# Fused high-weight matmul with a folded result, and every third low weight part on GpSimd

## The chip, the cores and the metric

The kernel runs on one core of a Trainium2 chip. The metric is the device time of one execution in microseconds (us); the time before is 1485.79 us, the median of three runs (1485.37 to 1486.06). Differences under 0.2% of it, 3 us, can hardly be told from no change.

Five engines work side by side, each through its own queue in order: TensorE (PE; its weight loads are listed as PEld), VectorE (DVE), ScalarE (ACT), GpSimd (POOL) and SyncE (SP), which here issues the DMAs. On-chip memory is SBUF, and PSUM for the results of matmuls; GpSimd works on SBUF alone in this kernel.

## The reference

Three transformer blocks on one sequence of 256 tokens with 1024 channels, all in float32: two layers of a first kind, one of a second. Cut to what matters:

```python
def first_block(x, ...):                      # two layers
    for l in range(2):
        h = rms_norm(x, norm1_g[l])
        (cq, ckv, kpe, gq, gk, gv, glr, gr, su, gates) = split_in(h @ w_in[l])     # 5808 columns
        o_a = mla_mixer(cq, ckv, kpe, ...)    # latent attention, 8 heads
        o_b = gla_mixer(gq, gk, gv, glr, gr, ...)   # gated linear attention
        o_c = s5_mixer(su, ...)               # state space scan, gelu, sigmoid-gated by y @ w_glu
        g = sigmoid(gates + gate_b[l]).reshape(B, L, 3, D)
        merged = g0 * (o_a @ w_br_mla) + g1 * (o_b @ w_br_gla) + g2 * (o_c @ w_br_s5)
        x = x + merged @ w_out[l]
        x = x + square(relu(rms_norm(x, norm2_g[l]) @ w_ff1[l])) @ w_ff2[l]        # 4096 hidden
def second_block(x, ...):                     # one layer
    q, k, v, glu_in, z_ga, z_gc = split(rms_norm(x, g_pre) @ w_in)
    y_attn = dilated_attention_mixer(q, k, v, rel_bias, w_attn_out)   # 3 groups of 8 heads
    y_conv = conformer_conv_mixer(glu_in, ...)   # glu, depthwise conv of width 31, norm, silu, w_conv_out
    x = x + rms_norm((sigmoid(z_ga) * y_attn + sigmoid(z_gc) * y_conv) @ w_mix_out)
    gate, up = split(rms_norm(x, g_pre_ffn) @ w_ffn_in)               # 2 x 2816
    x = x + rms_norm((silu(gate) * up) @ w_ffn_out)
```

## The kernel before

Every weight is read once, as a stream of 424 *units*. A unit is a tile `raw` of up to 128x1024 float32 (512 KB). To keep float32 accuracy, each unit is split into two parts of the type fp32r: ScalarE copies `raw` to the high part `wH` (`split`, L160), and VectorE subtracts to get the low part `wL = raw - wH` (L161). Activations are split in the same way (`hH` and `hL`, `fH` and `fL`, ...). A product of the two is three matmuls that add up in PSUM: high by high, high weight by low activation, low weight by high activation.

There are two kinds of product. In `mm_f` (L166) the weights are stationary, 128x128 at a time, and 256 tokens stream past: L169 (`hH` past `wH`), L170 (`hL` past `wH`), L171 (`hH` past `wL`). Output channels lie on partitions. A unit of `f_unit` has 8 such triples for 128 output channels: 24 matmuls of 256 columns into the first half of a PSUM tile `mm`. In `mm_t` (L173) the activations are stationary and 512 weight columns stream past (L175 to L177): the second matrices of the feed-forward parts (`ff2`, `ffo`), `w_out` and others, 12 matmuls of 512 columns to a unit.

The result of an `f_unit` is taken out of PSUM by its `evac`: mostly one ScalarE instruction that also does what comes next, as `Tanh` with a bias for the gates (`gate_evac`, L1038), `Relu` in the feed-forward part (`ff1`, L1190), `Tanh` or a bias for the two halves of the gated linear unit (`glu_gate` L1448, `glu_a` L1442). There are two `mm` tiles, taken in turn.

`fetch_` (L1773) issues a unit's DMA and its split; it runs three units ahead of the unit that is computed (`AHEAD`). The tile pools set what waits for what: three `raw` tiles, four `wH` and four `wL`, each taken in turn, so the DMA of unit i + 3 waits until the split of unit i has read `raw`, and the split of unit i + 4 until TensorE is done with unit i:

```python
    wraw = pool("wraw", 3)
    whl = pool("whl", 4)
    k.ps_mm = pool("ps_mm", 2, space=PS)
```

Twenty units have a factor per partition (`plan.scales`) and are split in two halves of 512 columns (L163, L164). The order of the units and of the side work beside them (the scan `s`, the attentions, the convolution `c`, the norms) stands in the tables `SCHED` and `SCHED2`. The convolution (`conv_gen`, L1250) is 31 taps over 256 tokens for eight channel tiles, on VectorE (`cv`, L1285 and L1278; ScalarE makes some products, `cvt`). GpSimd computes the powers -1/2 of the norms (`rsq`, L184) on at most 4 columns, and clears some tiles.

Of the kernel before, what the change touches and what calls it, by code (L numbers as in the profile page):

```python
# [150 lines left out]
def make(k, tc, ins, out, dbg=None):  # L151
    """Fills k with the helpers; returns the plan."""
# [132 lines left out]
def norm_full(k, t, rsn, ss, gb, dst):  # L285
    """rsn[:, t] = rsqrt(mean(x^2) + eps); the normed x into dst, transposed; gb holds g in every row."""
# [8 lines left out]

def row_tile(k, i, name):
# [5 lines left out]
def post_residual(k, t, accs, gb, eps=EPS * D):  # L302
    """x[:, t] += accs rsqrt(sum(accs^2) + eps) gb; gb holds sqrt(D) g."""
# [134 lines left out]
def s5_powers(k, st, name, nk, x, xs, ct, op):  # L438
    """[128, 8, nk, 16]: x times powers of lambda, for the four pairs of a channel tile, re and im."""
# [1502 lines left out]
```

## Time and profile before

| | |
|---|---|
| median of three runs | 1485.79 us |
| the profiled execution, span | 1482.4 us |
| PE busy | 1440.2 us (97%) |
| DVE busy | 1019.1 us (69%) |
| ACT busy | 840.1 us (57%) |
| POOL busy | 48.6 us (3%) |
| DMA | 243.13 MB, mean 164 GB/s |

The profile is of one execution; its own time is given as its span from the first to the last instruction, 1482.4 us, and the runs' median lies 3.4 us above that. In the rows below an instruction has the line of `kernel.py`, the engine, the tile that it writes and those that it reads, and its shape. Matmuls overlap in their records (one of 256 columns is shown as 0.28 us long, and the next one starts 0.12 us later), so a matmul's cost in a row of them is read from start to start. The same holds for VectorE, in a smaller measure.

### The profile page before, as it was taken

How to read it: one execution, taken by the hardware profiler on the slowest of the kernel's cores; microseconds unless marked ns; L12 is line 12 of the kernel's file. 1: busy time of each engine (PE TensorE's matmuls, PEld its weight loads, DVE VectorE, ACT ScalarE, POOL GpSimd, SP SyncE). 2: the span in 40 equal slices, each digit the busy share in tenths (PEclk: the TensorE clock that was granted, in tenths of full speed). 3: DMA queues.
4: the chain of work that ended last, by engine and by line, in shares of the span. 5: the costliest groups of instructions: out<-in, count | busy, mean ns of one | idle time of the engine just before them, and what ended most of it. 6: DMA issues, size and time to landing. Idle time of an engine off the chain costs nothing.

```text
span 1482.4 us, 26521 instructions
## 1 busy us (share of the span) xinstructions
PE 1440.2 (97%) x10580; PEld 1299.2 (88%) x10580; DVE 1019.1 (69%) x1876; ACT 840.1 (57%) x1469; POOL 48.6 (3%) x51
## 2 busy tenths in 40 slices
PE   8999999989999999989999999999999999899998
PEld 6979899778889899788988999989888989799997
DVE  7976777687455668566566555579988856765555
ACT  6855567465744556355546444465576574644443
POOL 1000100000000000012000000000000000000000
PEclk9999999999999999999999999999999999999999
DMA  6622344555455653235446555575544545355553
GB/s 223 207 86 97 108 162 152 163 171 183 160 165 186 209 165 94 81 130 171 155 164 218 189 185 186 188 234 178 179 146 121 167 143 206 126 195 185 185 185 114
DMA packets 71060, 243.13 MB, mean 164 GB/s; under 512 B 7864, under 2 KB 11656, under 8 KB 70936
## 3 DMA queue, kind: packets, MB, share of 16 engines
q1 hardware_dynamic: 70936, 241.43, 49.9%
q8 instruction: 83, 1.36, 0.4%
q14 instruction: 41, 0.34, 0.1%
HBM read 237.17 MB, written 4.23 MB: 163 GB/s over the span
## 4 chain that ended last, share of the span: by engine, by line
PE 72%; DVE 9%; ACT 3%; issue 2%; POOL 2%; DMA 1%; POOLq 0%; DVEq 0%; ACTq 0%; SPq 0%
PE mm L169 13%; PE mm L170 13%; PE mm L171 13%; PE acc L175 7%; PE acc L176 7%; PE acc L177 7%; DVE wL L161 3%; POOL rsq L184 2%; ACT wH L160 2%; DVE cv L1285 1%; PE acc L1409 1%; DMA raw<-in_wst_dram 1%; PE tr L1404 1%; PE acc L1382 1%; PE acc L548 1%
## 5 line engine op out<-in xcount | busy, mean ns | idle before, releaser
L161 DVE TENSOR_TENSOR wL<-raw,wH 128x1024 fp32r<-128x1024 f32 (+1 forms) x410 | 495.9, 1211 | 253.7 <-ACT wH L160 250.7
L160 ACT ACTIVATE wH<-raw 128x1024 fp32r<-128x1024 f32 (+1 forms) x410 | 429.2, 1047 | 379.7 <-PE mm L170 199.1
L169 PE MATMUL mm<-hH,wH 128*128 128x256 f32 x1920 | 553.5, 289 | 7.0 <-ACT gt L1038 3.5
L170 PE MATMUL mm<-hL,wH 128*128 128x256 f32 x1920 | 548.5, 286 | 3.2 <-DVE hL L164 3.2
L171 PE MATMUL mm<-hH,wL 128*128 128x256 f32 x1920 | 547.9, 286 | 0.0
L169 PEld LDWEIGHTS mm<-hH,wH 128*128 128x128 f32 x1920 | 368.5, 192 | 21.0 <-ACT hH L163 5.3
L170 PEld LDWEIGHTS mm<-hL,wH 128*128 128x128 f32 x1920 | 368.9, 192 | 8.8 <-DVE hL L164 4.4
L171 PEld LDWEIGHTS mm<-hH,wL 128*128 128x128 f32 x1920 | 368.9, 192 | 2.4 <-issue 1.9
L175 PE MATMUL acc<-wH,fH 128*128 128x512 f32 x344 | 135.3, 393 | 0.0
L176 PE MATMUL acc<-wL,fH 128*128 128x512 f32 x344 | 134.9, 392 | 0.0
L177 PE MATMUL acc<-wH,fL 128*128 128x512 f32 x344 | 134.1, 390 | 0.0
L1285 DVE SCALAR_TENSOR_TENSOR cv<-u,ppt,cv 128x256 f32<-128x256 f32 x184 | 78.6, 478 | 0.4
L177 PEld LDWEIGHTS acc<-wH,fL 128*128 128x128 f32 x344 | 64.6, 188 | 14.1
L175 PEld LDWEIGHTS acc<-wH,fH 128*128 128x128 f32 x344 | 64.9, 189 | 11.2
L176 PEld LDWEIGHTS acc<-wL,fH 128*128 128x128 f32 x344 | 64.9, 189 | 10.3
L160 ACT ACTIVATE fH<-ffr 128x256 fp32r<-128x256 f32 x64 | 26.6, 416 | 67.6 <-DVE ffr L1191 67.5
L161 DVE TENSOR_TENSOR fL<-ffr,fH 128x256 fp32r<-128x256 f32 x64 | 27.1, 424 | 23.2 <-ACT fH L160 23.2
L175 PE MATMUL acc<-wH,mH 128*128 128x512 f32 x96 | 37.9, 395 | 0.3 <-ACT mH L163 0.3
L176 PE MATMUL acc<-wL,mH 128*128 128x512 f32 x96 | 37.8, 394 | 0.0
L177 PE MATMUL acc<-wH,mL 128*128 128x512 f32 x96 | 37.2, 395 | 0.0
L184 POOL TENSOR_TENSOR rsq<-nm,mhalf 128x1 f32<-128x1 f32 x12 | 7.6, 635 | 841.5 <-DVE nm L223 841.5
L164 DVE SCALAR_TENSOR_TENSOR wL<-raw,ppt,wH 128x512 fp32r<-128x512 f32 x40 | 28.4, 747 | 9.1 <-ACT wH L163 9.1
(433 smaller groups left out, 2155.4 us busy)
## 6 DMA issues: line engine op xcount, KB each, us to landing
raw<-in_wst_dram SPq DMA_DIRECT2D x420, 512.0 KB, 3.4
xd<-x SPq DMA_DIRECT2D x6, 512.0 KB, 2.9
x<-xd SPq DMA_DIRECT2D x6, 512.0 KB, 4.3
bias<-bdram SPq DMA_DIRECT2D x8, 384.0 KB, 4.9
gnorm<-in_rows_dram SPq DMA_DIRECT2D x3, 512.0 KB, 5.1
raw<-in_wst_dram SPq DMA_DIRECT2D x4, 384.0 KB, 4.1
x<-in_x_dram SPq DMA_DIRECT2D x4, 256.0 KB, 3.3
x<-in_x_dram SPq DMA_DIRECT2D x2, 512.0 KB, 5.1
```

Source lines behind the costliest of these rows:

```text
L160: nc.scalar.activation(H, src, AF.Copy)
L161: nc.vector.tensor_sub(L, src, H)
L164: nc.vector.scalar_tensor_tensor(L, src, scale, H.bitcast(F32), op0=OP.mult, op1=OP.subtract)
L169: nc.tensor.matmul(ps, H[:, w], aH[:, i, :], start=(i == 0), stop=False)
L170: nc.tensor.matmul(ps, H[:, w], aL[:, i, :], start=False, stop=False)
L171: nc.tensor.matmul(ps, L[:, w], aH[:, i, :], start=False, stop=(i == nk - 1))
L175: nc.tensor.matmul(ps, aH[:, ki, tt], H[:, cols], start=start, stop=False)
L176: nc.tensor.matmul(ps, aH[:, ki, tt], L[:, cols], start=False, stop=False)
L177: nc.tensor.matmul(ps, aL[:, ki, tt], H[:, cols], start=False, stop=stop)
L184: nc.gpsimd.tensor_tensor(o, m, k.mhalf[:, 0:1].to_broadcast([P, n]), op=OP.pow)
L548: nc.tensor.matmul(ps[:, (4 * c + q) * 64:(4 * c + q + 1) * 64], E[:, c, :], us[:, q, :], start=True, stop=True)
L1285: nc.vector.scalar_tensor_tensor(st.cv[:, ct], u(ct, i), w(ct, i), st.cv[:, ct], op0=OP.mult, op1=OP.add)
```

## The change

`mm_p` takes the place of `mm_f` in all `f_unit`s, in the small unit `kg`, in the convolution's output and in the gate of the scan branch. The high and the low part of an activation now lie side by side in one tile (`h[:, i]` is 2 x 256 columns), and one matmul of 512 columns streams both past the high weights, into the two halves of the PSUM tile. The low weights add to the first half. `fold` then adds the halves: ScalarE copies the second half to SBUF (with the bias, where there is one), VectorE adds the first. What was one instruction on ScalarE with a function is now `fold` and the function after it. Scales of 1/8 are moved to where they cost nothing.

Of the weight units, every third one (number i with i mod 3 = 1) that has no factors gets its low part from GpSimd instead of VectorE. `SCHED`, `SCHED2`, the pools and the order of the weights stay. `mm_f` stays for the three branch matrices and the attention's output, `mm_t` as it was.

```diff
+    def mm_p(ps, H, L, a, nk, off=0, m=P):
+        for i in range(nk):
+            w = slice((off + i) * m, (off + i + 1) * m)
+            ai = a(i)
+            nc.tensor.matmul(ps, H[:, w], ai.rearrange("p b n -> p (b n)"), start=(i == 0), stop=False)
+            nc.tensor.matmul(ps[:, :S], L[:, w], ai[:, 0], start=False, stop=(i == nk - 1))
+
+    def fold(out, ps, bias=None, view=lambda a: a):
+        if bias is None:
+            nc.scalar.activation(out, view(ps[:, S:]), AF.Copy)
+        else:
+            nc.scalar.activation(out, view(ps[:, S:]), AF.Identity, bias=bias)
+        nc.vector.tensor_add(out, view(ps[:, :S]), out)
...
 def new_h(k):
-    hH = k.act.tile([P, 8, S], F32R, tag="hH", name="hH")
-    hL = k.act.tile([P, 8, S], F32R, tag="hL", name="hL")
-    return hH, hL
+    return k.act.tile([P, 8, 2, S], F32R, tag="h", name="h")
...
 def f_unit(k, plan, st, blocks, evac, nk=8):
     def run(H, L):
         ps = k.mm_tile()
-        k.mm_f(ps[:, :S], H, L, st.hH, st.hL, nk)
+        k.mm_p(ps, H, L, lambda i: st.h[:, i], nk)
...
-            nc.scalar.activation(st.gt[b, n // 2][:, n % 2], ps[:, :S], AF.Tanh, scale=0.5,
-                                 bias=k.pp("gateb", l)[:, i:i + 1])
+            g = st.gt[b, n // 2][:, n % 2]
+            k.fold(g, ps)
+            nc.scalar.activation(g, g, AF.Tanh, scale=0.5, bias=k.pp("gateb", l)[:, i:i + 1])
...
     def ff1(n):
         def evac(ps):
             r = k.t1("ffr")
-            nc.scalar.activation(r, ps[:, :S], AF.Relu)
-            nc.vector.tensor_mul(r, r, r)
+            k.fold(r, ps)
+            nc.vector.scalar_tensor_tensor(r, r, 0.0, r, op0=OP.max, op1=OP.mult)
...
+LOW_POOL = 3
...
+        elif i % LOW_POOL == 1:
+            nc.scalar.activation(H[:, :n], raw[:, :n], AF.Copy)
+            nc.gpsimd.tensor_tensor(L[:, :n], raw[:, :n], H[:, :n].bitcast(F32), op=OP.subtract)
         else:
             k.split(H[:, :n], L[:, :n], raw[:, :n])
```

TensorE's order inside an `f_unit`, where `h` is the activations' tile, before:

```order
L169 MATMUL mm<-hH,wH 128x256
L170 MATMUL mm<-hL,wH 128x256
L171 MATMUL mm<-hH,wL 128x256
L169 MATMUL mm<-hH,wH 128x256
L170 MATMUL mm<-hL,wH 128x256
L171 MATMUL mm<-hH,wL 128x256
```

and now:

```order
L179 MATMUL mm<-h,wH 128x512
L180 MATMUL mm<-h,wL 128x256
L179 MATMUL mm<-h,wH 128x512
L180 MATMUL mm<-h,wL 128x256
```

Three matmuls of 256 columns became one of 512 and one of 256; all in all TensorE has 2016 matmuls fewer (1920 of the units on `h`, 64 of the convolution's output, 32 of the scan's gate).

VectorE's order where the convolution runs beside the units of the gated linear unit (`u` is that unit's result, `cv` the sum over the taps), before:

```order
L161 TENSOR_TENSOR wL<-raw,wH 128x1024
L1451 SCALAR_TENSOR_TENSOR u_11242<-g2th,ga 128x256
L1285 SCALAR_TENSOR_TENSOR cv<-u_11173,ppt,cv 128x256
L1285 SCALAR_TENSOR_TENSOR cv<-u_11104,ppt,cv 128x256
L1285 SCALAR_TENSOR_TENSOR cv<-u_11173,ppt,cv 128x256
L1282 TENSOR_SCALAR cv<-u_11242,ppt 128x256
L161 TENSOR_TENSOR wL<-raw,wH 128x1024
L1278 TENSOR_TENSOR cv<-cvt,cv 128x512
```

and now:

```order
L161 TENSOR_TENSOR wL<-raw,wH 128x1024
L1480 SCALAR_TENSOR_TENSOR u_10386<-g2th,ga 128x256
L188 TENSOR_TENSOR ga<-mm,ga 128x256
L1313 SCALAR_TENSOR_TENSOR cv<-u_10218,ppt,cv 128x256
L1313 SCALAR_TENSOR_TENSOR cv<-u_10162,ppt,cv 128x256
L1313 SCALAR_TENSOR_TENSOR cv<-u_10218,ppt,cv 128x256
L188 TENSOR_TENSOR g2th<-mm,g2th 128x256
L1306 TENSOR_TENSOR cv<-cvt,cv 128x512
L1313 SCALAR_TENSOR_TENSOR cv<-u_10274,ppt,cv 128x256
L1480 SCALAR_TENSOR_TENSOR u_10442<-g2th,ga 128x256
```

A `wL` is missing between the two `u`s (GpSimd has it), and the adds of `fold` (L188) stand among the taps.

GpSimd's order in the second half of the first layer (`rsq` are powers for the attention's norms), before:

```order
L184 TENSOR_TENSOR rsq_2051<-qss,mhalf 128x4
L184 TENSOR_TENSOR rsq_2068<-qss,mhalf 128x4
L184 TENSOR_TENSOR rsq_2201<-kss,mhalf 128x4
L184 TENSOR_TENSOR rsq_2222<-kss,mhalf 128x4
```

and now:

```order
L1817 TENSOR_TENSOR wL<-raw,wH 128x1024
L201 TENSOR_TENSOR rsq_1914<-qss,mhalf 128x4
L201 TENSOR_TENSOR rsq_1931<-qss,mhalf 128x4
L1817 TENSOR_TENSOR wL<-raw,wH 128x1024
L201 TENSOR_TENSOR rsq_2058<-kss,mhalf 128x4
L201 TENSOR_TENSOR rsq_2079<-kss,mhalf 128x4
```

The powers now stand behind low parts: 136 of them (135 of 1024 columns, one of 384) on a queue that had 35 powers.

## Rows read from the trace of the kernel before

**Rows 1.** The page: span, and busy time of each engine with its instructions

```profile
span 1482.4 us, 26521 instructions
...
PE 1440.2 (97%) x10580; PEld 1299.2 (88%) x10580; DVE 1019.1 (69%) x1876; ACT 840.1 (57%) x1469; POOL 48.6 (3%) x51
```

**Rows 2.** The page: the chain that ended last, by engine

```profile
PE 72%; DVE 9%; ACT 3%; issue 2%; POOL 2%; DMA 1%; POOLq 0%; DVEq 0%; ACTq 0%; SPq 0%
```

**Rows 3.** Busy time by stage: stretch, length, engines, clock, DMA share, GB/s

```profile
995.00:1065.00 70.00, 69.45 (x493) 65.31 (x493) 68.12 (x123) 43.97 (x70) 0.00 (x0) 1.00 0.58 186
1065.00:1200.00 135.00, 134.36 (x983) 118.35 (x981) 115.55 (x273) 86.30 (x161) 1.68 (x1) 1.00 0.47 144
800.00:960.00 160.00, 160.00 (x1029) 146.15 (x1029) 91.52 (x114) 76.79 (x115) 0.00 (x0) 1.00 0.57 188
```

**Rows 4.** Timeline of PE, feed-forward part: start us, length us, engine, line

```profile
801.99 0.40 PE L175 MATMUL acc<-wH,fH 128*128 128x512 f32 x1
...
804.74 0.28 PE L169 MATMUL mm<-hH,wH 128*128 128x256 f32 x1
...
807.61 0.40 PE L175 MATMUL acc<-wH,fH 128*128 128x512 f32 x1
```

**Rows 5.** Timeline of PE, where w_out alternates with a branch matrix

```profile
762.82 0.40 PE L175 MATMUL acc<-wH,mH 128*128 128x512 f32 x1
...
768.28 0.28 PE L169 MATMUL mm<-moH,wH 128*128 128x256 f32 x1
...
771.16 0.40 PE L175 MATMUL acc<-wH,mH 128*128 128x512 f32 x1
```

**Rows 6.** Matmuls of L169 alone, in the stages of rows 3 (PE, PEld)

```profile
995.00:1065.00 70.00, 37.22 (x132) 25.29 (x132) 1.00 0.58 186
1065.00:1200.00 135.00, 71.99 (x251) 47.76 (x250) 1.00 0.47 144
```

**Rows 7.** Timeline of DVE in the convolution

```profile
1008.34 1.22 DVE L161 TENSOR_TENSOR wL<-raw,wH 128x1024 fp32r<-128x1024 f32 x1
1009.47 0.42 DVE L1451 SCALAR_TENSOR_TENSOR u<-g2th,ga 128x256 f32<-128x256 f32 x1
1009.81 1.67 DVE L1285 SCALAR_TENSOR_TENSOR cv<-u,ppt,cv 128x256 f32<-128x256 f32 x4
```

**Rows 8.** The tile raw from 995 to 1065: count, ns min/median/max

```profile
L161 DVE TENSOR_TENSOR wL<-raw,wH x25: 1211/1217/1226, 993.9 to 1062.8; 128x1024 fp32r<-128x1024 f32 x25
```

**Rows 9.** DVE's groups from 995 to 1200: count, busy us, mean ns, idle before

```profile
L161 DVE TENSOR_TENSOR wL<-raw,wH 128x1024 fp32r<-128x1024 f32 x57 | 69.4, 1220 | 8.7 <-ACT wH L160 6.9 <-PE mm L171 1.6
```

**Rows 10.** Groups of ACT: count, busy us, mean ns, idle before

```profile
L160 ACT ACTIVATE wH<-raw 128x1024 fp32r<-128x1024 f32 (+1 forms) x410 | 429.2, 1047 | 379.7 <-PE mm L170 199.1 <-issue 118.6 <-PE acc L177 33.2
L1038 ACT ACTIVATE gt<-mm,ppt 128x256 f32<-128x256 f32 x48 | 22.2, 463 | 3.1 <-PE mm L171 3.0
```

**Rows 11.** Timeline of POOL: two clears, and three powers

```profile
1.62 1.81 POOL L1674 MEMSET s5w<- 128x2048 f32 x1
3.36 0.95 POOL L1675 MEMSET s5ep<- 128x1024 f32 x1
...
219.50 1.85 POOL L184 TENSOR_TENSOR rsq<-qss,mhalf 128x4 f32<-128x4 f32 x1 [2.81 <-DVE qss L822]
228.36 1.01 POOL L184 TENSOR_TENSOR rsq<-kss,mhalf 128x4 f32<-128x4 f32 x1 [7.01 <-DVE kss L845]
...
497.67 0.56 POOL L184 TENSOR_TENSOR rsq<-nm,mhalf 128x1 f32<-128x1 f32 x1 [263.33 <-DVE nm L223]
```

**Rows 12.** Timeline of DVE beside those powers

```profile
219.26 1.22 DVE L161 TENSOR_TENSOR wL<-raw,wH 128x1024 fp32r<-128x1024 f32 x1
...
228.51 1.23 DVE L161 TENSOR_TENSOR wL<-raw,wH 128x1024 fp32r<-128x1024 f32 x1
```

**Rows 13.** The tile raw from 800 to 960: min/median/max, and landing of its DMAs

```profile
L160 ACT ACTIVATE wH<-raw x57: 1044/1057/1059, 799.4 to 956.9; 128x1024 fp32r<-128x1024 f32 x57
...
DMA to landing us min/median/max: 3.0/3.3/5.2
```

More of the change, by code (lines that the diff above doesn't have):

```diff
@@ L123 @@
 class K:
+    pass
 def bcm(ap, n):
@@ L293, in norm_full, with pair4, split4 @@
         transpose_half(k, t, q, xn, None, dst)
+def pair4(k, name):
+    return [k.t4(name, (P, 2, 2, S), F32R) for _ in range(2)]
+def split4(k, pair, src, scale=None):
+    for i, t in enumerate(pair):
+        k.split(t[:, :, 0], t[:, :, 1], src[:, 2 * i:2 * i + 2], scale)
 def row_tile(k, i, name):
@@ L630, in s5_glu_tile @@
     ps = k.mm_tile()
-    k.mm_f(ps[:, :S], H, L, st.gH, st.gL, 4, off)
+    k.mm_p(ps, H, L, lambda i: st.gp[i // 2][:, i % 2], 4, off)
     th = k.t1("gluth")
-    nc.scalar.activation(th, ps[:, :S], AF.Tanh, scale=0.5, bias=st.hb[:, n:n + 1])
+    k.fold(th, ps)
+    nc.scalar.activation(th, th, AF.Tanh, scale=0.5, bias=st.hb[:, n:n + 1])
     o4 = k.t1("o4")
@@ L1003, in run @@
                 st.su = k.t4("su", (P, 4, 4, 64))
-            nc.scalar.activation(st.su[:, n], ps[:, :S].rearrange("p (n s) -> p s n", s=4), AF.Copy)
+            k.fold(st.su[:, n], ps, view=lambda a: a.rearrange("p (n s) -> p s n", s=4))
         return run
@@ L1008, in kg_evac, with gqk_evac @@
         st.kg = k.t1("kg")
-        nc.scalar.activation(st.kg[0:64], ps[0:64, :S], AF.Copy)
-    def gqk_evac(name, n, scale):
+        k.fold(st.kg[0:64], ps[0:64])
+    def gqk_evac(name, n):
         def run(ps):
@@ L1014, in run @@
                 setattr(st, name, k.t2(name, (P, 2, S)))
-            nc.scalar.activation(getattr(st, name)[:, n], ps[:, :S], AF.Copy, scale=scale)
+            k.fold(getattr(st, name)[:, n], ps)
         return run
@@ L1021, in run @@
             L = k.main.tile([P, 1, S], F32R, tag="lat", name=name + "L")
-            k.split(H[:, 0], L[:, 0], ps[:, :S], k.pp(gname, l)[:, n:n + 1])
+            x = k.t1("latx")
+            k.fold(x, ps)
+            k.split(H[:, 0], L[:, 0], x, k.pp(gname, l)[:, n:n + 1])
             getattr(st, name + "H")[n] = H
@@ L1230, in norm1 @@
             spill_x(k, t)
[L1231 removed]
+        nx.h = h
         k.dump_x(f"x{l}b")
@@ L1335, in conv_ln @@
     yield
-    st.cH = [k.t4("cH", (P, 4, S), F32R) for _ in range(2)]
-    st.cL = [k.t4("cL", (P, 4, S), F32R) for _ in range(2)]
+    st.cp = [pair4(k, "cp") for _ in range(2)]
     for h, c in enumerate(cv):
@@ L1441, in evac @@
             st.ga = k.t1("ga")
-            nc.scalar.activation(st.ga, ps[:, :S], AF.Identity, bias=k.pp("bglua")[:, i:i + 1])
+            k.fold(st.ga, ps, k.pp("bglua")[:, i:i + 1])
         f_unit(k, plan, st, f_blocks("w_in_2", 0, A0 + i * P, 8), evac)
@@ L1447, in evac @@
             th = k.t1("g2th")
-            nc.scalar.activation(th, ps[:, :S], AF.Tanh, scale=0.5, bias=k.pp("bglug")[:, i:i + 1])
+            k.fold(th, ps)
+            nc.scalar.activation(th, th, AF.Tanh, scale=0.5, bias=k.pp("bglug")[:, i:i + 1])
             u = k.main.tile([P, 30 + S], F32, tag="u", name=f"u{i}")
@@ L1469, in evac @@
                 d[n // 2] = k.main.tile([P, 2, S], F32, tag="gt", name="z")
-            nc.scalar.activation(d[n // 2][:, n % 2], ps[:, :S], AF.Tanh, scale=0.5)
+            z = d[n // 2][:, n % 2]
+            k.fold(z, ps)
+            nc.scalar.activation(z, z, AF.Tanh, scale=0.5)
         f_unit(k, plan, st, f_blocks("w_in_2", 0, c0 + n * P, 8), evac)
@@ L1500, in run @@
             ps = k.mm_tile()
-            for i in range(8):
-                w = slice(i * P, (i + 1) * P)
-                cH, cL = st.cH[i // 4][:, i % 4], st.cL[i // 4][:, i % 4]
-                nc.tensor.matmul(ps[:, :S], H[:, w], cH, start=(i == 0), stop=False)
-                nc.tensor.matmul(ps[:, :S], H[:, w], cL, start=False, stop=False)
-                nc.tensor.matmul(ps[:, :S], L[:, w], cH, start=False, stop=(i == 7))
+            k.mm_p(ps, H, L, lambda i: st.cp[i // 4][i % 4 // 2][:, i % 2], 8)
             x = k.t1("cox")
-            nc.scalar.activation(x, ps[:, :S], AF.Identity, bias=k.pp("bconv")[:, n:n + 1])
+            k.fold(x, ps, k.pp("bconv")[:, n:n + 1])
             z = zc[n // 2][:, n % 2]
@@ L1575, in evac @@
             s = k.t1("ffs")
-            nc.vector.tensor_mul(s, ps[:, :S], st.rsB)
+            k.fold(s, ps)
+            nc.vector.tensor_mul(s, s, st.rsB)
             nc.scalar.activation(s, s, AF.Silu)
@@ L1583, in evac @@
             s = sg.pop(i)
-            nc.vector.tensor_tensor(s, ps[:, :S], s, op=OP.mult)
+            u = k.t1("ffup")
+            k.fold(u, ps)
+            nc.vector.tensor_mul(s, u, s)
             hH = k.t1("fH", (P, 1, S), F32R)
```

50 lines of the change are left out of this document (24 added, 26 removed).

## The prediction

> **What bounds the kernel now.** I read the page first: TensorE is busy for 97% of the span, VectorE for 69%, ScalarE for 57%, GpSimd for 3% [rows 1]. Matmul records overlap, so 97% alone proves little; the chain of waits bears it out, with 72% of its length on TensorE and 9% on VectorE [rows 2]. Then the busy times by stage. In the feed-forward part (800 to 960 us) TensorE has no idle time, at a granted clock of 1.00, and VectorE is busy for 91.5 of 160 us. Beside the convolution it is different: from 995 to 1065 us VectorE is busy for 68.1 of 70 us, from 1065 to 1200 us for 115.6 of 135, while TensorE too stays at 69.5 and 134.4 [rows 3]. So the kernel is bound by the stream of matmuls, and for the 70 us in the convolution by two engines at once. The reader is to see there that a faster TensorE is worth its whole gain in the feed-forward part, and next to nothing where VectorE is full.
>
> **TensorE.** The columns that stream do not change: 3 x 256 before, 512 + 256 now. What can go is a fixed cost per matmul, and two sizes side by side show it. In the feed-forward part 12 matmuls of 512 columns take 804.74 - 801.99 = 2.75 us, 229.2 ns each, and 24 of 256 columns take 807.61 - 804.74 = 2.87 us, 119.6 ns each [rows 4]. Two of 256 are thus 2 x 119.6 - 229.2 = 10.0 ns dearer than one of 512. Where w_out alternates with a branch matrix it is 24 of 512 in 5.46 us (227.5 ns) and 24 of 256 in 2.88 us (120.0 ns), a difference of 12.5 ns [rows 5]. 2016 pairs become one matmul each: 20.2 us by the first, 25.2 us by the second; I take 11 ns, 22.2 us. A unit of `f_unit` falls from 2.87 to 2.78 us.
>
> The Trainium skill speaks against this term: "TensorE: Matmul & The Clock Gate", section "Wait — 56ns, not 53.3ns?", gives a warm matmul N / 2.4 GHz plus about 2.5 ns. By it the 2016 matmuls would be worth 5 us. The trace disagrees: 256 columns at 2.4 GHz are 106.7 ns and the row shows 119.6 to 120.0, so about 13 ns are fixed here [rows 4, 5].
>
> **VectorE's own work.** 135 low parts of 1024 columns go; one takes 1009.47 - 1008.34 = 1.13 us from start to start: -153 us. 256 adds of `fold` come, on 128x256: 1009.81 - 1009.47 = 0.34 us each [rows 7], +87 us. Net -66 us, all of it beside TensorE's stream, so worth nothing by itself except in the convolution.
>
> **ScalarE.** The copies of `fold` stand where an evacuation stood. The functions behind them are new: some 80 `Tanh` of about 0.46 us, by the row of the gates, 37 us on an engine that is 57% busy and that waits 199 us for TensorE ahead of its `wH` alone [rows 1, 10]. Hidden: cost 0. Without that cover it would be the 37 us.
>
> **GpSimd's low part.** No row has it. The widest work of GpSimd is a clear: 2048 columns in 3.36 - 1.62 = 1.74 us, 0.87 us for 1024, which reads nothing; a power on one column takes 0.56 us [rows 11]. Bounds: 0.87 us from below; from above two reads and a write one after another and the fixed part, 3 x 0.87 + 0.56 = 3.2 us. I take two passes, 2 x 0.87 + 0.56 = 2.3 us. (A power on four columns takes 1.01 us [rows 11], and by its 0.15 us a column a low part would take 156 us; I exclude that end, since a subtraction is no power.) 136 x 2.3 = 313 us, 21% of the span.
>
> Is it in time? The low part of unit i must be there when TensorE is done with unit i - 1, and ScalarE can start `wH` when it is done with unit i - 4: three units, 8.35 us, for 1.06 + 2.3 us. The ring of the `raw` tile is tighter: with three tiles and every third unit, GpSimd always has the same one. From one `wH` to the next in it lie 1.06 us, GpSimd's part, 3.3 us (3.0 to 5.2) from the DMA's issue to landing [rows 13], and three hand-overs, about 0.1 us together: 4.5 us plus GpSimd's part, against 8.35 us. It holds up to 3.8 us, waits included. Cost 0.
>
> **The hold between VectorE and GpSimd.** At 219.26 us a low part starts on VectorE; a power that GpSimd starts at 219.50 takes 1.85 us. The same power at 228.36 us takes 1.01 us [rows 11, 12]. The first one waited until VectorE's subtraction was through. The other way round nothing is seen: VectorE's low part that starts at 228.51, inside the power, takes its usual 1.23 us [rows 12]. But that power reads 4 columns, and now GpSimd reads 1024. So the bounds of what one GpSimd part costs VectorE are 0 and its whole 2.3 us.
>
> In the Trainium skill, "SBUF — State Buffer", section "Who interferes with whom", a VectorE instruction with two inputs in SBUF and a GpSimd instruction that reads SBUF exclude each other, and the one that starts first holds the port for its whole length. Rows 11 and 12 agree for a VectorE that came first; no row shows the other order at this size.
>
> Priced where VectorE is full. From 995 to 1065 us there are 25 low parts [rows 8], 8.3 for GpSimd, and 132 triples, 16.5 units [rows 6]. VectorE: 68.1 - 8.3 x 1.13 + 16.5 x 0.34 = 64.3 us, and TensorE wants 70 - 132 x 0.010 = 68.7 us: room for 4.4 us, against a hold of 0 to 8.3 x 2.3 = 19.1 us. From 1065 to 1200 us there are 57 - 25 = 32 low parts [rows 9], 10.7 for GpSimd, and 251 triples, 31.4 units [rows 6]: 115.6 - 12.1 + 10.7 = 114.2 us of 132.5, room for 18.3, hold 0 to 24.6 us. The taps, the products and the low parts all read two tiles of SBUF, so an instruction to be held is mostly there. The full hold costs 14.7 + 6.3 = 21 us, half of it 9.6 - 4.4 = 5.2 us and nothing. I take the half, +5 us: the only row with GpSimd first is nearest to zero, the rows with VectorE first are at the whole. Elsewhere VectorE has the room.
>
> **Powers behind low parts.** 35 powers now share the queue with work for 21% of the time, each on average 0.21 x 1.15 = 0.24 us later, 8.5 us. The chain has about 2% of the span on GpSimd, some 30 of its 49 us [rows 1, 2]; I count half of the delay: +4.3 us (0, if the powers fall between, to 8.5).
>
> **Sum**, against the profiled 1482.4 us: -22.2 + 5.2 + 4.3 = -12.7 us, 1469.7 us. The runs' median lies 3.4 us above the span, so 1473 us.
>
> **Rivals.**
> - *No hold.* Then the 5 us are not lost and the second row's 25.2 us may be had: 1485.8 - 25.2 + 0 to 4 = 1460 to 1468 us. For it: the undisturbed 1.23 us of rows 12. Against: the 1.85 us of rows 11.
> - *The full hold, which ends slower.* Place: units of `f_unit` back to back outside the feed-forward parts. These are 256 - 108 = 148 units, a third of them, 49, with a GpSimd part. In the convolution it costs the 21 us above. In the other 33 the adds of `fold` stand behind a held instruction, and the `mm` tile comes free late: 0.46 us of copy, 2.3 of hold, 0.34 of add and 0.1 of hand-overs are 3.2 us, while with two tiles TensorE waits beyond one unit, 2.78 us: 33 x 0.4 = 13 us. Sum: -22 + 21 + 13 + 4 = +16 us, 1502 us. It decides from a hold of some 88% of 2.3 us; at 80% the tile is free in time (2.74 us), the convolution costs 10.9 + 1.4 us, and the sum is -22 + 12 + 4 = -6 us, 1480 us.
> - *The fixed cost stays*, because it hangs on the streamed columns or on the way that the sizes alternate: then TensorE gains nothing, and 0 to 9.5 us of hold and powers are added: 1486 to 1495 us. Against it: two stages apart, each with a difference of 10 ns or more. By the Trainium skill's 2.5 ns a matmul (the section above) it would end 5 us lower.
> - *The ring of `raw`.* If a GpSimd part with its wait takes 4.5 us, the ring takes 9.0 us against 8.35, and the 194 units of the feed-forward parts, 65 rings, cost 42 us: 1506 us. For it only the far end of the landings.
>
> **How the numbers follow.** Forecast, the hold near the half: 0.40, with its own range 1467 to 1481 us. No hold: 0.27. Full hold or close to it: 0.20, of which 0.12 slower, 0.04 unchanged, 0.04 still faster. Fixed cost stays: 0.08, half of it unchanged, half slower. The ring: 0.05, 0.04 slower and 0.01 unchanged. Faster by over 0.2% (3 us): 0.40 + 0.27 + 0.04 = 0.71 (3 us is about what a measurement can tell from no change); within: 0.09; slower: 0.20. The range holds the forecast, nearly all of the first rival and the lower part of the second: 1458 to 1494 us.
>
> **What would show it.** In the profile after: pairs of 512 and 256 columns that start 349 ns apart, against 3 x 119.6 = 359 (the fixed cost; 354 or more and the third rival is right). The `wL` of GpSimd at 2.3 us alone and longer behind VectorE. VectorE's taps between 995 and 1200 us: idle time or longer records beside GpSimd's parts show the hold, and TensorE's waits there for `wL` or for a VectorE add are its price. The feed-forward stretches should be shorter by 3%, with TensorE still full: if it waits for a `wL` of GpSimd or `raw` there, the ring is it. The forecast is wrong above all if a GpSimd part is far from 2.3 us.

## The result, and the profile after

The changed kernel takes 1560.9 us (median of 4 runs) against 1485.6 us for the kernel before: 1.0508 times as long, 95% interval 1.0484 to 1.0531. The prediction was 1473 us, range 1458 to 1494: wrong in its direction, and the time lies 67 us above the range.

The page after: span, busy times, and the chain that ended last.

```profile
span 1558.3 us, 22947 instructions
...
PE 1452.9 (93%) x8564; PEld 1194.2 (77%) x8564; DVE 1140.6 (73%) x2000; ACT 884.3 (57%) x1607; POOL 374.8 (24%) x187
...
PE 46%; DVE 8%; ACT 2%; issue 1%; POOL 1%; DMA 0%; POOLq 0%; DVEq 0%; ACTq 0%
```

Against [rows 1, 2]: TensorE is idle for 1558.3 - 1452.9 = 105 us where it was 42. VectorE's busy time has risen by 121 us; I had predicted that its work falls by 66. (The chain can be followed over 58% of the span here and over 89% before, so its shares are not compared.) Where an engine's busy time rises though its work falls, look at the means of single shapes. These are groups of the page after (the columns as in [rows 9]).

```profile
L1817 POOL TENSOR_TENSOR wL<-raw,wH 128x1024 fp32r<-128x1024 f32 x136 | 335.9, 2470 | 1018.2 <-ACT wH L1816 885.2
...
L161 DVE TENSOR_TENSOR fL<-ffr,fH 128x256 fp32r<-128x256 f32 x64 | 63.6, 993 | 30.0 <-ACT fH L160 30.0
...
L1219 DVE SCALAR_TENSOR_TENSOR ffr<-ffr 128x256 f32<-128x256 f32 x64 | 56.4, 882 | 1.9
L188 DVE TENSOR_TENSOR ffr<-mm,ffr 128x256 f32<-128x256 f32 x64 | 26.8, 419 | 29.6 <-ACT ffr L185 29.6
```

Three VectorE instructions of the same size, 128x256, in the same unit of the feed-forward part: the two that read both operands from SBUF take 993 and 882 ns on average, the add of `fold`, which reads one from PSUM, 419. In the kernel before, the same `fL` took 424 ns:

```profile
L161 DVE TENSOR_TENSOR fL<-ffr,fH 128x256 fp32r<-128x256 f32 x64 | 27.1, 424 | 23.2 <-ACT fH L160 23.2
```

The timelines of VectorE and of GpSimd over the same microseconds of the changed kernel, at two places, show why.

```profile
477.15 0.42 DVE L188 TENSOR_TENSOR ffr<-mm,ffr 128x256 f32<-128x256 f32 x1 [1.40 <-ACT ffr L185]
...
849.70 2.43 DVE L161 TENSOR_TENSOR fL<-ffr,fH 128x256 fp32r<-128x256 f32 x1 [0.48 <-ACT fH L160]
...
853.41 0.42 DVE L161 TENSOR_TENSOR fL<-ffr,fH 128x256 fp32r<-128x256 f32 x1 [0.48 <-ACT fH L160]
```
```profile
476.98 2.39 POOL L1817 TENSOR_TENSOR wL<-raw,wH 128x1024 fp32r<-128x1024 f32 x1 [5.89 <-ACT wH L1816]
...
849.46 2.38 POOL L1817 TENSOR_TENSOR wL<-raw,wH 128x1024 fp32r<-128x1024 f32 x1 [9.73 <-ACT wH L1816]
```

The `fL` that starts inside GpSimd's part at 849.46 us ends 0.29 us after it (852.13 against 851.84 us); the next one, alone, takes 0.42 us. The add of `fold` at 477.15 us lies inside a part too and takes its usual 0.42 us. So the hold is whole, not half. The Trainium skill ("SBUF — State Buffer", section "Who interferes with whom") says that two SBUF inputs contend with a GpSimd instruction that reads SBUF, that at most one does not outside VectorE's 2-port modes, and that whoever comes first has the port for the whole instruction. The trace agrees for GpSimd's low parts: 2.43 us with two SBUF inputs, 0.42 us with one. It does not for a GpSimd power of four columns, inside which VectorE's low part takes its usual 1.23 us [rows 11, 12].

The second loss needs no low part on GpSimd. Timelines of GpSimd, VectorE and TensorE, in which TensorE waits for `fold`'s add:

```profile
197.36 1.97 POOL L201 TENSOR_TENSOR rsq<-kss,mhalf 128x4 f32<-128x4 f32 x1 [3.33 <-DVE kss L870]
```
```profile
197.24 1.23 DVE L642 TENSOR_TENSOR s5w<-s5w,s5y 128x1024 f32<-128x1024 f32 x1
199.36 0.23 DVE L873 TENSOR_SCALAR krc<-rsq,mla_rs 128x4 f32<-128x4 f32 x1 [0.90 <-POOL rsq L201]
199.50 0.29 DVE L876 TENSOR_TENSOR mla_kn<-kr,rsq 128x128 f32<-128x128 f32 x1
199.70 0.42 DVE L875 TENSOR_TENSOR mla_kn<-acc,krc 128x256 f32<-128x256 f32 x1
200.04 0.41 DVE L188 TENSOR_TENSOR gt<-mm,gt 128x256 f32<-128x256 f32 x1
```
```profile
200.51 0.53 PE L179 MATMUL mm<-h,wH 128*128 128x512 f32 x1 [3.95 <-DVE gt L188]
```

VectorE stands at `krc` for a power, which itself takes 1.97 us and not 1.01, since `s5w` of VectorE is under way when it starts (so did a power before, 1.85 us [rows 11]); the add of a gate, which alone can free an `mm` tile, is queued three instructions behind. TensorE waits for 3.95 us. Before, ScalarE freed this tile with the gate's `Tanh`. Five of TensorE's eight largest groups of waits after (us in total, times, longest) are for VectorE, two of them for `fold`'s add:

```profile
PE acc L606 <- DVE s5z L593: 10.2, 4, 3.9
PE tr L922 <- DVE mla_p L918: 9.0, 5, 5.3
PE mm L179 <- DVE gt L188: 7.1, 4, 4.0
...
PE mm L179 <- DVE su L188: 4.5, 1, 4.5
```

Third, a wait is paid again behind it. The one shown here begins with a held instruction of another kind: `rsq`, a `TENSOR_SCALAR` on 128x4, takes 2.33 us inside a GpSimd part where it takes 0.23 at 243.75 us, and the transposes `tr` of the attention wait for what is computed from it (VectorE, GpSimd, TensorE). At most 2.1 of the 4.04 us are that hold.

```profile
248.97 2.33 DVE L849 TENSOR_SCALAR rsq<-rsq,mla_rs 128x4 f32<-128x4 f32 x1 [0.53 <-POOL rsq L201]
```
```profile
248.90 2.37 POOL L1817 TENSOR_TENSOR wL<-raw,wH 128x1024 fp32r<-128x1024 f32 x1
```
```profile
254.55 0.53 PE L891 MATMUL tr<-cst,mla_qn 128*96 128x128 f32 x3 [4.04 <-DVE mla_qn L858]
```

Busy times (PE, PEld, DVE, ACT, POOL) and granted clock around this wait:

```profile
252.50:254.50 2.00, 0.00 (x0) 0.00 (x0) 2.00 (x7) 0.08 (x1) 0.00 (x0) 1.00 0.05 8
254.50:256.50 2.00, 1.95 (x10) 1.72 (x11) 1.20 (x8) 0.66 (x2) 1.02 (x1) 0.73 0.90 309
256.50:258.50 2.00, 2.00 (x8) 1.71 (x7) 2.00 (x5) 0.87 (x2) 0.00 (x0) 0.50 0.51 207
258.50:260.50 2.00, 2.00 (x16) 1.90 (x15) 1.25 (x5) 0.98 (x2) 0.67 (x1) 0.91 0.37 66
```

TensorE did nothing for 4.04 us, and in the three stretches of 2 us that follow its mean granted clock was 0.73, 0.50 (1.2 GHz, the lower of the two levels) and 0.91. Over the span the mean granted clock is 0.978, before 0.992:

```profile
core 0: 1558.3 us, clock 0.978
```

That is 0.022 x 1558 = 34 us of full speed missing, before 0.008 x 1482 = 12. TensorE's idle time grew by 63 us and its busy time by 13, though it has 2016 matmuls fewer; that is the 76 us by which the span grew. The clock's 22 us are contained in these.

### The profile page after: what moved, and what is told of

It reads as the page before. It is cut to its first block, busy times and chain, and to the rows that moved or that the text cites. A ratio compares the mean times of both kernels' runs of the same rounds, so it can differ in the third digit from the quotient of the medians.

```text
span 1558.3 us, 22947 instructions
## 1 busy us (share of the span) xinstructions
PE 1452.9 (93%) x8564; PEld 1194.2 (77%) x8564; DVE 1140.6 (73%) x2000; ACT 884.3 (57%) x1607; POOL 374.8 (24%) x187
## 4 chain that ended last, share of the span: by engine, by line
PE 46%; DVE 8%; ACT 2%; issue 1%; POOL 1%; DMA 0%; POOLq 0%; DVEq 0%; ACTq 0%
PE mm L179 16%; PE mm L180 8%; PE acc L192 4%; PE acc L194 4%; PE acc L193 4%; DVE cv L1313 2%; DVE wL L161 2%; PE mm L171 1%; PE mm L169 1%; PE mm L170 1%; PE acc L1437 1%; ACT wH L160 1%; PE acc L1410 1%; PE tr L1432 1%; DVE cv L1306 1%
## 5 line engine op out<-in xcount | busy, mean ns | idle before, releaser
L179 PE MATMUL mm<-h,wH 128*128 128x512 f32 x1920 | 711.6, 409 | 31.4 <-DVE h L164 6.9
L1817 POOL TENSOR_TENSOR wL<-raw,wH 128x1024 fp32r<-128x1024 f32 x136 | 335.9, 2470 | 1018.2 <-ACT wH L1816 885.2
L180 PE MATMUL mm<-h,wL 128*128 128x256 f32 x1920 | 550.5, 287 | 0.0
L179 PEld LDWEIGHTS mm<-h,wH 128*128 128x128 f32 x1920 | 366.9, 191 | 132.1 <-DVE h L164 9.2
L161 DVE TENSOR_TENSOR wL<-raw,wH 128x1024 fp32r<-128x1024 f32 (+1 forms) x274 | 334.5, 1221 | 141.7 <-ACT wH L160 141.0
L160 ACT ACTIVATE wH<-raw 128x1024 fp32r<-128x1024 f32 (+1 forms) x274 | 285.6, 1043 | 173.3 <-PE mm L179 64.5
L180 PEld LDWEIGHTS mm<-h,wL 128*128 128x128 f32 x1920 | 369.6, 193 | 8.2 <-issue 3.7
L1816 ACT ACTIVATE wH<-raw 128x1024 fp32r<-128x1024 f32 x136 | 143.4, 1055 | 123.0 <-PE mm L179 50.7
L1219 DVE SCALAR_TENSOR_TENSOR ffr<-ffr 128x256 f32<-128x256 f32 x64 | 56.4, 882 | 1.9
L188 DVE TENSOR_TENSOR ffr<-mm,ffr 128x256 f32<-128x256 f32 x64 | 26.8, 419 | 29.6 <-ACT ffr L185 29.6
L1603 DVE TENSOR_TENSOR ffs<-ffs,rsB 128x256 f32<-128x256 f32 x22 | 40.2, 1828 | 0.8
```

Of the source, the lines that this page charges most:

```text
L160: nc.scalar.activation(H, src, AF.Copy)
L161: nc.vector.tensor_sub(L, src, H)
L179: nc.tensor.matmul(ps, H[:, w], ai.rearrange("p b n -> p (b n)"), start=(i == 0), stop=False)
L180: nc.tensor.matmul(ps[:, :S], L[:, w], ai[:, 0], start=False, stop=(i == nk - 1))
L1219: nc.vector.scalar_tensor_tensor(r, r, 0.0, r, op0=OP.max, op1=OP.mult)
L1603: nc.vector.tensor_mul(s, s, st.rsB)
```

## The experiments

All times are medians. The kernel before had 1486.2 to 1487.3 us on the same chips.

**fold alone.** The changed kernel, all low parts on VectorE: `elif i % LOW_POOL == LOW_POOL:`, never true.

> The changed kernel with all low weight parts on VectorE again; the fused matmul and fold stay. Theory H (GpSimd's reads hold VectorE, and that is the loss): the loss goes, 1470 to 1495 us. Theory R (the add of fold puts the release of the two PSUM tiles on VectorE's queue, behind waiting instructions): most of the loss stays, 1530 to 1560 us, though no low part is on GpSimd.

Measured: 1538.3 us, ratio 1.0344 [1.0324, 1.0364]. That is the range of theory R: `fold` without GpSimd costs 52 us, of a change predicted to gain. TensorE's first wait is now

```profile
PE mm L179 <- DVE z L188: 8.9, 4, 5.5
```

**GpSimd alone.** The kernel before, with GpSimd's third of the low parts:

```diff
+        elif i % 3 == 1:
+            nc.scalar.activation(H[:, :n], raw[:, :n], AF.Copy)
+            nc.gpsimd.tensor_tensor(L[:, :n], raw[:, :n], H[:, :n].bitcast(F32), op=OP.subtract)
```

> The kernel before with every third low part on GpSimd, nothing else changed. Theory H: 1530 to 1560 us, the VectorE instructions with two SBUF inputs stretched by about 1.5 us for each GpSimd part. Theory R: 1485 to 1500 us, since ScalarE still empties the PSUM tiles.

Measured: 1581.4 us, ratio 1.0641 [1.0599, 1.0682]: 95 us, more than both theories said. On top of `fold` the same low parts cost 1560.9 - 1538.3 = 23 us; there they also take work off a VectorE that `fold` has loaded (44 us, by the next run). The first to the last matmul on `fH` or `fL`, in the three feed-forward parts, take 198.8, 173.6 and 175.3 us against 184.3, 172.7 and 175.4: where VectorE only serves the feed-forward units the low parts on GpSimd are nearly free (+0.9, -0.1), and they cost 14.5 us in the first, where VectorE makes the next layer's scan matrices beside them. There the hold goes the other way. From 360.70 to 370.01 us VectorE has one instruction with two SBUF inputs behind the other, and a GpSimd part that starts among them takes 11.04 us and not 2.4; TensorE then waits for this low part (GpSimd, TensorE).

```profile
361.17 11.04 POOL L1787 TENSOR_TENSOR wL<-raw,wH 128x1024 fp32r<-128x1024 f32 x1 [6.50 <-DVE fL L161]
```
```profile
372.26 0.79 PE L176 MATMUL acc<-wL,fH 128*128 128x512 f32 x1 [6.21 <-POOL wL L1787]
```

**GpSimd clears instead.** The changed kernel with three clears per part, which leaves out every third low part.

```diff
-            nc.gpsimd.tensor_tensor(L[:, :n], raw[:, :n], H[:, :n].bitcast(F32), op=OP.subtract)
+            for _ in range(3):
+                nc.gpsimd.memset(L[:, :n].bitcast(F32), 0.0)
```

> The changed kernel, where GpSimd clears its wL three times (about 2.7 us, as long as the subtraction) in place of subtracting: it reads nothing, so a hold on SBUF reads can't occur, while lateness, queue and order stay. It leaves out every third low weight part. Theory H: 1475 to 1500 us, no stretched VectorE records. Theory R: 1535 to 1560 us, as the changed kernel or little less.

Measured: 1493.8 us, ratio 1.0050 [1.0035, 1.0066]. That is in theory H's range. GpSimd is busy for longer than in the changed kernel (428.9 us against 374.8), and VectorE's instructions with two SBUF inputs are not held (timelines of GpSimd and VectorE; 0.42 us is the time alone):

```profile
318.99 2.98 POOL L1818 MEMSET wL<- 128x1024 f32 x3 [10.01 <-PE mm L180]
```
```profile
320.13 0.42 DVE L1219 SCALAR_TENSOR_TENSOR ffr<-ffr 128x256 f32<-128x256 f32 x1
```

VectorE's busy time is 964.7 us here against 1140.6. Small `TENSOR_SCALAR` instructions are held by a clear as well (the `rsq` of 128x4 takes 0.89 us at 226.66 us, alone 0.23), so a little of the hold is left in this run. So 1560.9 - 1493.8 = 67 us hang on GpSimd's subtraction. The clears do not wait for `wH`, so this run alone does not exclude that late low parts are a share of it.

**No add.** `fold` as one ScalarE copy of the first half, all low parts on VectorE: high weight x low activation is left out.

> The changed kernel with all low parts on VectorE, and in place of fold one ScalarE copy of the first half (the high weights by the low activations are left out of the result, though still computed). ScalarE alone empties the PSUM tile again. Both theories: about 2016 x 9 ns = 18 us below the kernel before, 1465 to 1478 us. If it stays above 1485 us, the fused matmul itself is at fault (theory M).

Measured: 1488.6 us, ratio 1.0017 [1.0003, 1.0031]. The other 50 us of `fold` are its add. And without the add the fused matmul still gains nothing, where 1465 to 1478 us were expected.

**Release by ScalarE.** All low parts on VectorE, and in `fold`:

```diff
+        half = k.t1("half")[0:ps.shape[0]]
+        nc.scalar.activation(half, ps[:, :S], AF.Copy)
...
-        nc.vector.tensor_add(out, view(ps[:, :S]), out)
+        nc.vector.tensor_add(out, view(half), out)
```

> The changed kernel with all low weight parts on VectorE again, and fold with one step more: ScalarE copies both halves out of the mm tile (about 256 copies more of 0.42 us, 108 us on an engine busy for some 880 us), VectorE adds the two copies in SBUF, so VectorE no longer releases the mm tile. Theory R (fold alone cost 52 us because the add that frees the mm tile stands in VectorE's queue behind instructions that wait): 1484 to 1500 us, and the TensorE stalls of about 4 us behind a VectorE add are gone. Rival L (the adds make the gates, the convolution's inputs and the rest late, whoever frees the tile): 1525 to 1545 us, like fold alone. If ScalarE becomes the bound instead: over 1500 us with TensorE waiting for ScalarE's copies.

Measured: 1523.1 us, ratio 1.0242 [1.0220, 1.0265]: 15 us less than `fold` alone. My theory R fails as the whole cause: the late release is a part.

**The same copies without the add** (line `tensor_add` taken out, the second half's copy read by no one; high weight x low activation is left out).

> The kernel in which ScalarE copies both halves out, but without VectorE's add: the first half alone is the result, the copy of the second half is read by no one (high weight x low activation is left out). All low parts on VectorE. Theory V (ScalarE's second copy is hidden, so that the 37 us of the run with copies and add are the add itself, its time and its place in VectorE's queue): 1485 to 1495 us. Rival S (the second copies load ScalarE until it sets the pace, and release by VectorE was the whole cost of fold): 1510 to 1525 us.

Measured: 1493.5 us, ratio 1.0053 [1.0033, 1.0072]. Theory V holds: ScalarE's second copies cost 5 us over the run without add (1488.6). So the release through VectorE was worth about 15 + 5 = 20 us, and 1523.1 - 1493.5 = 30 us remain for an add that frees nothing.

**Adds for no one.** The kernel before, with one add on constants behind each unit:

```diff
             evac(ps)
+            nc.vector.tensor_add(k.dummy, k.cst[:, 0:S], k.cst[:, 0:S])
```

> The kernel before, with one more VectorE add of 128x256 behind each of the 238 units of f_unit, on constants in SBUF and for no one: nobody waits for its result, no PSUM tile hangs on it, and nothing is left out. Theory V (fold's add costs above all by the 0.34 to 0.42 us of VectorE that it takes, in stages where VectorE's chain sets the pace): 1505 to 1525 us, most of the 37 us that fold with ScalarE's release cost. Rival R (only the wait in VectorE's queue and the late release cost, VectorE has room): 1485 to 1492 us.

Measured: 1501.4 us, ratio 1.0091 [1.0066, 1.0116], just under theory V's interval. The group of VectorE:

```profile
L974 DVE TENSOR_TENSOR dummy<-cst 128x256 bf16<-128x256 f32 x238 | 100.3, 421 | 3.6
```

100 us of VectorE work for no one cost 15 us of time. If the shares add up, about 20 of the 50 us of `fold`'s add are then the late release, 15 VectorE's time, and some 15 are left for results that come late in VectorE's queue; that last share is a remainder, not measured by itself.

**Quarters.** GpSimd alone, each part as four subtractions of 256 columns:

```diff
+                for c in (slice(0, 256), slice(256, 512), slice(512, 768), slice(768, 1024)):
+                    nc.gpsimd.tensor_tensor(L[:, c], raw[:, c], H[:, c].bitcast(F32), op=OP.subtract)
```

> The kernel before with every third low part on GpSimd, as in the run that cost 95 us, but each part as four subtractions of 256 columns. Theory H (a GpSimd instruction that reads SBUF holds VectorE for its own whole length, and VectorE gets in between two of them): a hold is at most about 0.65 us instead of 2.4, 1495 to 1535 us. Rival H2 (VectorE gets in only when GpSimd's queue has nothing more to do, or the cost hangs on the sum of GpSimd's time): 1575 to 1595 us, as with whole parts.

Measured: 1571.6 us, ratio 1.0568 [1.0542, 1.0593], against 1581.4 with whole parts: my H is wrong, and H2 is 3 us off. VectorE is held for less: 0.85 us here in place of 0.42, until the first quarter of four ends (VectorE, then GpSimd).

```profile
479.65 0.85 DVE L1191 TENSOR_TENSOR ffr<-ffr 128x256 f32<-128x256 f32 x1 [1.53 <-ACT ffr L1190]
```
```profile
479.48 3.23 POOL L1789 TENSOR_TENSOR wL<-raw,wH 128x256 fp32r<-128x256 f32 x4 [5.43 <-ACT wH L1786]
```

But a VectorE that has one instruction with two SBUF inputs behind the other keeps a quarter out as it kept the whole part: one quarter takes 9.42 us while VectorE's instructions from 363.50 to 372.81 us have their usual length, and TensorE waits for the low part. (GpSimd, one of VectorE, TensorE.)

```profile
363.97 9.42 POOL L1789 TENSOR_TENSOR wL<-raw,wH 128x256 fp32r<-128x256 f32 x1 [5.10 <-ACT wH L1786]
```
```profile
367.51 1.22 DVE L1791 TENSOR_TENSOR wL<-raw,wH 128x1024 fp32r<-128x1024 f32 x1
```
```profile
374.13 0.80 PE L176 MATMUL acc<-wL,fH 128*128 128x512 f32 x1 [5.30 <-POOL wL L1789]
```

A GpSimd quarter takes 872 ns on average over 540, and 0.72 undisturbed: 82 us more in all, where the whole parts took 28 us more (136 x (2.60 - 2.39)). VectorE's busy time is 940.9 us against 990.4. So shorter pieces move about 50 us of hold from one engine to the other, and 10 of the 95 us of time are won.

**Copies on GpSimd.** The changed kernel with `nc.gpsimd.tensor_copy(L[:, :n], raw[:, :n])` in place of the subtraction; the raw weight stands where every third low part was.

> The changed kernel, with GpSimd copying raw to wL (one input of 128x1024 in SBUF) in place of the subtraction (two inputs): the low part of every third unit is left out of the result, the raw weight stands in its place. Theory T (only a GpSimd instruction with two inputs in SBUF holds VectorE): 1488 to 1500 us, as when GpSimd only cleared wL. Rival A (any wide GpSimd instruction that reads SBUF holds it): 1540 to 1565 us, as in the changed kernel.

Measured: 1510.5 us, ratio 1.0155 [1.0132, 1.0179], between both. Theory T falls: one input is enough (VectorE, GpSimd).

```profile
380.23 1.19 DVE L1219 SCALAR_TENSOR_TENSOR ffr<-ffr 128x256 f32<-128x256 f32 x1
```
```profile
380.09 1.04 POOL L1817 CAST wL<-raw 128x1024 fp32r<-128x1024 f32 x1 [8.13 <-PE acc L193]
```

The hold is as long as the GpSimd instruction, 1.04 us here and 2.38 with two inputs: it costs 17 us over the clears, not 67.

**Reads beside.** The kernel before, GpSimd doing the four quarters into a small tile while VectorE still makes every low part.

> The kernel before, with GpSimd doing the four subtractions of 256 columns beside, into a small tile that no one reads: VectorE still makes every low part, so no low part can be late through GpSimd, and nothing is left out; only the raw tile is held until GpSimd is through. Theory H (what costs is that VectorE and GpSimd keep each other from running): 1570 to 1650 us, as much as with the low parts made by GpSimd, or more, since VectorE has 153 us more to do. Rival Q (the cost of GpSimd's low parts was that they came late): 1486 to 1500 us.

Measured: 1689.4 us, ratio 1.1353 [1.1318, 1.1389], above even theory H. Late low parts of GpSimd are excluded as this run's cause, but it does not isolate the hold either: GpSimd's quarter grows to 1232 ns, four are 4.9 us, the `raw` tile is kept for so long that the ring of `raw` goes over, and `raw` stands in the chain:

```profile
PE 28%; POOL 23%; DMA 15%; DVE 11%; ACT 8%; issue 5%; ACTq 0%; POOLq 0%; SPq 0%; DVEq 0%
```

Of how the 95 us of GpSimd alone divide between the held VectorE and low parts that come late since GpSimd itself was held, I have only the waits: TensorE waits for 13.2 us for `wL` of GpSimd there, in the changed kernel for 3.2 (first row: GpSimd alone).

```profile
PE acc L176 <- POOL wL L1787: 13.2, 3, 6.2
```
```profile
PE acc L193 <- POOL wL L1817: 3.2, 2, 2.3
```

**The matmul alone.** The kernel before with the new layout and `mm_p` in `f_unit` and `kg`, each evacuation as it was from `ps[:, :S]`; high weight x low activation is left out. And its control, the layout with `mm_f`, which leaves nothing out.

> The kernel before, with nothing but the fused matmul in f_unit and in the kg unit (about 1920 pairs), and each evacuation as it was, from the first half alone: high weight x low activation is left out of the result. No add, no extra Tanh step, nothing on GpSimd. Theory M (a fused pair saves about 9 ns in its own unit, and the 512-column matmuls beside it give part of it back; stages outside the feed-forward part wait for something else): 1477 to 1484 us. The prediction's 11 ns kept whole (1920 x 11 ns = 21 us): 1463 to 1467 us. No gain at all, as in the run with the add replaced by a copy: 1485 to 1489 us.

> The kernel before with the new layout of the activations alone (high and low part side by side in one tile h), and three matmuls of 256 columns as before. If the layout and the order that it brings are free: 1484 to 1488 us, and then the fused matmul by itself gains nothing against three. If they cost what the fused matmul gains (theory O): 1495 to 1507 us, and the fused matmul is worth some 10 to 20 us against this kernel.

Measured: 1486.8 us, ratio 1.0003 [0.9990, 1.0015], and 1484.9 us, ratio 0.9993 [0.9978, 1.0007]. 1920 matmuls fewer gain nothing, and the layout is not what eats it. In the changed kernel's feed-forward part it can be seen (TensorE; a unit of `f_unit`, then one with `fH`):

```profile
882.55 0.39 PE L179 MATMUL mm<-h,wH 128*128 128x512 f32 x1
...
885.36 0.40 PE L192 MATMUL acc<-wH,fH 128*128 128x512 f32 x1
...
888.14 0.39 PE L179 MATMUL mm<-h,wH 128*128 128x512 f32 x1
```

The fused unit takes 2.81 us, 351 ns a pair where 349 were predicted. But the 12 matmuls of 512 columns behind it now take 2.78 us instead of 2.75 [rows 4]. Both together: 5.59 us against 5.62, so half of the 0.06 us is left.

**Sizes apart.** The same kernel, a unit's eight matmuls of 512 first and its eight of 256 behind them (the loop of `mm_p` split in two).

> The kernel with nothing but the fused matmul in f_unit and the kg unit, evacuated from the first half alone (high weight x low activation is left out), with each unit's 512-column matmuls first and its 256-column ones behind them. Theory A (alternating sizes cost what the fused matmul gains): the feed-forward stretches at 183, 170 and 172 us, and 4 to 10 us less than with alternating sizes: 1476 to 1483 us; less than the 21 us of 1920 x 11 ns, since the other stages wait for VectorE and ScalarE. If the stages between set the pace alone, 1484 to 1488 us; if the 11 ns come everywhere, 1464 to 1468 us.

Measured: 1480.5 us, ratio 0.9964 [0.9948, 0.9980]. Theory A holds in the main: the feed-forward parts take 181.9, 169.6 and 171.4 us (before 184.3, 172.7, 175.4; with alternating sizes 184.5, 172.0, 173.0). Alternating sizes cost 6.6 of the 9.5 us that the fused matmul gains there.

**Feed-forward only.** `fold` and the fused matmul in the feed-forward parts, all low parts on VectorE.

```diff
+        if fused:
+            k.mm_p(ps, H, L, lambda i: st.h[:, i], nk)
+        else:
+            k.mm_f(ps[:, :S], H, L, st.h[:, :, 0], st.h[:, :, 1], nk)
```

> The kernel before with the fused matmul and fold in the three feed-forward parts alone (108 units, 864 pairs), all low parts on VectorE; nothing is left out. From the feed-forward stretches of the fold-only run (183.3, 171.2 and 173.4 us against 184.3, 172.7 and 175.4): 4.5 us less, 1480 to 1483 us. By the prediction's 11 ns a pair: 9.5 us less, 1476 us. If fold's add stalls TensorE there too: over 1486 us.

Measured: 1485.3 us, ratio 0.9993 [0.9980, 1.0006]. The feed-forward parts gain 4.2 us as expected (183.6, 171.3, 173.3); the kernel gains nothing clear of noise, and misses the 1480 to 1483 us. A part of the difference, some 1 us, is the first unit: a fused matmul needs both halves of `h`, and waits for VectorE's low half, in the first of these parts for 0.89, 0.30, 0.47 and 0.26 us before, 1.9 in all, and for 2.8 here (TensorE). Where the rest goes no run shows.

```profile
301.95 0.50 PE L177 MATMUL mm<-h,wH 128*128 128x512 f32 x1 [1.16 <-DVE h L164]
303.60 0.50 PE L177 MATMUL mm<-h,wH 128*128 128x512 f32 x1 [1.03 <-DVE h L164]
305.85 0.61 PE L177 MATMUL mm<-h,wH 128*128 128x512 f32 x1 [0.64 <-DVE h L164]
```

**The better version.** The same, sizes apart, and the first unit of each part with three matmuls (`fused=n > 0`).

> The fused matmul in the three feed-forward parts alone, as before, with two edits: the eight matmuls of 512 columns of a unit come first and the eight of 256 behind them, and the first unit of each feed-forward part keeps its three matmuls, so that it need not wait for the low half of h. Nothing is left out. If a part of the fixed cost hangs on the way that the sizes alternate: a unit of 8 x (229 + 119) = 2.78 us and no dearer 512 columns behind it, the stretch of layer 1's feed-forward part (first to last matmul on fH or fL) at 169 to 170 us instead of 171.3, 1475 to 1480 us. If not: 171.3 us again, and only the first units' waits of 1.3 us each are saved, 1480 to 1484 us. If neither: 1485 us.

Measured: 1478.7 us, ratio 0.9944 [0.9927, 0.9961]: 0.6% below the kernel before. The unit and its neighbour:

```profile
873.65 1.98 PE L177 MATMUL mm<-h,wH 128*128 128x512 f32 x8
875.46 1.12 PE L181 MATMUL mm<-h,wL 128*128 128x256 f32 x8
876.42 0.40 PE L189 MATMUL acc<-wH,fH 128*128 128x512 f32 x1
...
879.16 1.98 PE L177 MATMUL mm<-h,wH 128*128 128x512 f32 x8
```

2.77 us for the unit and 2.74 for the 12 behind it, 5.51 against 5.62 before; layer 1's feed-forward part takes 169.9 us.

## Why the prediction was wrong, step by step

In a chain of the runs: fused matmul alone 1486.8, with one copy of `fold` 1488.6 (+2), with its add 1538.3 (+50), with a third of the low parts off VectorE and nothing that reads on GpSimd 1493.8 (-44), with GpSimd's subtraction 1560.9 (+67). Two steps of the prediction failed above all, the price of VectorE's own work and the hold.

- **"VectorE's own work ... worth nothing by itself except in the convolution": failed.** I read slack from a mean busy share (57 to 69%). The add costs 50 us and taking low parts off gives 44 back. In the profiled executions `fold` alone is longer than the kernel before by 27 us ahead of the first feed-forward part, 8 between the first and the second and 25 between the second and the third, and shorter by 4.5 us in the three. In the stages between, VectorE runs chains of short dependent instructions, and an instruction queued behind a waiting one waits too. Even adds that no one waits for cost 15 us.
- **"The hold ... I take the half": failed, and was the largest.** It is whole (2.43 us beside a part of 2.38), the upper of the two bounds. 5 us predicted, 67 measured (95 without `fold`). I priced it in the convolution alone, because "elsewhere VectorE has the room". There it is 21 us: from the first to the last start of an instruction of the taps 199.1 us, with clears 178.5. The rest lies elsewhere: 27 us ahead of the first feed-forward part, 8 in it, 10 between it and the second (the profiled execution against that with clears). The row that I gave the most weight, the low part at 228.51 us inside a power of four columns [rows 11, 12], shows that such a power does not hold VectorE; it could not show what 1024 columns do. VectorE's hold on GpSimd, up to 11.04 us for one part, stood in no term.
- **The rival of the full hold** had the mechanism, the side and the 21 us of the convolution, but 1502 us: it counted 0.4 us a unit for a late `mm` tile, while single waits are 4 us long, since the add stands behind an attention chain that itself waits for GpSimd.
- **The `mm` tile's release** was priced only under the hold; it costs about 20 us without GpSimd.
- **TensorE, -22 us: failed in size as the change does it.** The 11 ns are there when sizes do not alternate: with sizes apart layer 1's feed-forward part gains 172.7 - 169.6 = 3.1 us over the 29 units, 232 pairs, that lie in it, 13 ns each. Alternating, two thirds of the gain are taken back; the third rival named this and got 0.08. In the other stages the stream does not set the end: sizes apart gain 9.5 us in the feed-forward parts and 5.8 in the kernel.
- **Powers behind low parts, +4.3 us:** not borne out as worked out. One of the 35 powers stands behind a low part and starts 2.5 us after the `qss` that it reads; the others start within 0.14 us of theirs. What the one costs no run shows.

```profile
241.72 1.99 POOL L201 TENSOR_TENSOR rsq<-qss,mhalf 128x4 f32<-128x4 f32 x1
```

- **The clock** stood in no term: waits behind which TensorE works at 1.2 GHz.
- **A sum:** the first rival's upper end of 1468 us needs the 22.2 us; with the 25.2 that it names it would be 1465.
- **Right:** GpSimd's part, 2.3 us predicted, 2.39 alone (2.47 on average); ScalarE's new functions at next to nothing (+2 us); the ring of `raw`, not the limit until GpSimd holds it for 4.9 us (over the 3.8 allowed).

## What to carry to other kernels

An engine at 60 to 70% has no room by that alone: where it runs a dependent chain, every instruction added to its queue, and every buffer whose release is moved into that queue, can end up on the path. GpSimd instructions that read SBUF are not a free helper beside a VectorE that works on SBUF pairs; price the whole GpSimd instruction as a hold of either engine. Cutting it in four won back 10 of 95 us here. Matmuls fused to save a fixed cost should be ordered so that equal sizes stand together.

## What was not expected

Alternating 512 and 256 columns makes the 512-column matmuls behind them dearer too (2.78 against 2.75 us for 12), and grouping them gives 0.08 us a pair of units back (5.51 against 5.59); why, no run shows. And a VectorE that never pauses can stretch a GpSimd part of 2.4 us to 11.04 us.
